# Moving two small table loads of a rotary-embedding kernel to ScalarE's DMA queue, each in three parts

## The chip, the cores and the metric

The kernel runs on one core of a Trainium2 chip. The metric is the device time of one execution in microseconds (us), as the median of several runs. The span in a profile is some 2 us shorter than that time (160.8 against 162.55 us in the profiled run of the kernel before).

## The reference, cut to what matters

```python
x = x.reshape(batch, seq, num_heads, head_dim)       # 16, 512, 16, 64; float32
x1, x2 = x[..., :32], x[..., 32:]
rotated = concatenate([x1 * cos - x2 * sin, x1 * sin + x2 * cos], axis=-1)
```

x and the result have 33.55 MB each; cos and sin have 512 x 32 values, 64 KB each. The arithmetic is small beside the 67 MB that go in and out.

## The kernel before

x is cut into 8 tiles of 128 partitions x 8,192 values (4 MB). A tile is loaded, rotated in place and stored, and SyncE (SP) issues every load and store on its own queue. Five tile buffers are used in turn. The start, where the change lies:

```python
FIRST = (3, 8)                       # tile 0 is loaded in two parts: 3 and 5 row blocks
...
load(0, 0, FIRST[0])                 # SP: x tile 0, part 1: 12,288 bytes a partition
sin_sb = bp.tile(...)[:64, :256]
cos_sb = bp.tile(...)[:64, :256]
nc.sync.dma_start(out=sin_sb, in_=sin_v)   # 64 rows of 1,024 bytes
nc.sync.dma_start(out=cos_sb, in_=cos_v)
for lo, hi in zip(FIRST, FIRST[1:]):
    load(0, lo, hi)                  # x tile 0, part 2: 20,480 bytes a partition
for t in range(1, BUFS):
    load(t)                          # x tiles 1 to 4: 32,768 bytes a partition
...
# both batches of a tile use the same 64 table rows: PE copies them to 128 partitions
nc.tensor.matmul(out=sin_t, lhsT=spread, rhs=sin_sb, ...)
nc.tensor.matmul(out=cos_t, lhsT=spread, rhs=cos_sb, ...)
nc.vector.tensor_scalar_mul(out=sns[:, :, 0, :], in0=sin_k, scalar1=-1.0)
nc.vector.tensor_copy(out=sns[:, :, 1, :], in_=sin_k)
... # then all of VectorE's and POOL's work on x, which needs both tables
```

The x products with cos and most sums are VectorE's (DVE in the profile), 7 of 8 products with sin are POOL's, and PE with ScalarE (ACT) does a quarter of the sums.

Of the kernel before, what the change touches and what calls it, by code (L numbers as in the profile page):

```python
# [27 lines left out]
def kernel(  # L28
# [13 lines left out]
    nc = tc.nc  # L42
# [12 lines left out]
    cos_v = cos.rearrange("(p k) j -> p (k j)", k=KK)  # L55
    sin_v = sin.rearrange("(p k) j -> p (k j)", k=KK)
# [22 lines left out]
    load(0, 0, FIRST[0])  # L79
    sin_sb = bp.tile([P, dim], FP32, name="b")[:PB, : KK * half]  # L80
    cos_sb = bp.tile([P, dim], FP32, name="b")[:PB, : KK * half]
    nc.sync.dma_start(out=sin_sb, in_=sin_v)
    nc.sync.dma_start(out=cos_sb, in_=cos_v)
    for lo, hi in zip(FIRST, FIRST[1:]):
        load(0, lo, hi)
    for t in range(1, BUFS):
# [27 lines left out]
    def cos_b(k, n):  # L114
        c = cos_t[:, k * half : (k + 1) * half]
        return bass.AP(tensor=c.tensor, offset=c.offset, ap=[c.ap[0], [0, n], [1, half]])
# [17 lines left out]
    def pairs(r):  # L134
        return r.rearrange("p (a j) -> p a j", j=half)
# [21 lines left out]
    for t in range(NT):  # L157
        xt = tiles[t]
        for k in range(KK):
# [6 lines left out]
            if k in PE_ROWS[t % 2]:  # L166
                parts = []
                for c in range(0, dim, BANK):
# [3 lines left out]
                        out=pairs(ps), in0=pairs(rc), in1=cos_b(k, BANK // half), op=ALU.mult  # L172
# [51 lines left out]
```

## Time and profile before

| | before |
|---|---|
| median time | 162.58 us (162.51 to 162.78, 5 runs beside the changed kernel) |
| first and last movement of data (packet records) | 1.74 and 159.37 us after the span's start |
| sin, cos landed | 7.6 and 8.0 us |
| first VectorE product on x | 10.90 us |
| last store issued | 152.1 us |

Two bounds have nearly the same height. The DMA engines always have data to move, and VectorE works without a stop from 10.90 us to its end at 152.07 us. The lines are in the prediction below. Throughout, "packet records" are the trace's list of single DMA transfers: one entry for each contiguous row (1,024, 12,288, 20,480 bytes and so on) and one of 4 bytes for each completion signal of a DMA engine. The records don't name the DMA engine; where medians over the 16 engines are given, packets of one size were taken sixteen at a time in order of start.

The times of packet records in the prediction and in the expectations were counted from a point 0.24 us before the start that the timeline uses: 1.98, 6.33 and 159.6 us there are 1.74, 6.10 and 159.4 us on the timeline's clock. Outside those texts this document gives all packet times on the timeline's clock.

### The profile page before, as it was taken

The numbers are of one execution on the slowest core, as the hardware profiler recorded it, in microseconds if no ns is written. First come the engines' busy times: TensorE is split into PE (matmuls) and PEld (weight loads), VectorE is DVE, ScalarE is ACT, GpSimd is POOL, SyncE is SP. The second block draws the span as 40 slices with busy tenths as digits, with TensorE's granted clock in tenths as the row PEclk, the third lists the DMA queues.
The fourth block names the chain that finished last, engine by engine and source line by source line (L and its number), as shares of the span: only waits on it lengthen the run. The fifth ranks groups of instructions, "written<-read, shape, count | busy, mean of one in ns | idle before, by whom it ended". The sixth has DMA issues, their size and how long they took to land. (4 is left out here: it accounts for less than half of the span.)

```text
span 160.8 us, 524 instructions
## 1 busy us (share of the span) xinstructions
PE 62.3 (39%) x71; PEld 20.0 (12%) x71; DVE 141.4 (88%) x142; ACT 20.0 (12%) x33; POOL 130.3 (81%) x62
## 2 busy tenths in 40 slices
PE   3045380546217260708035440918053721735000
PEld 0022020202011110202020200211020201111000
DVE  1059999999999999999999999999999999999800
ACT  0110220021102020111102020112002110202000
POOL 1039999999999999999999899999999799950000
PEclk9999958576956755595555555555955585587655
DMA  5999999999999999999999999999999999999994
GB/s 186 395 423 463 408 481 416 391 497 416 391 489 416 402 416 481 408 391 505 399 399 481 424 399 475 424 408 432 465 399 432 465 408 432 457 416 408 428 428 179
DMA packets 2754, 67.26 MB, mean 418 GB/s; under 512 B 320, under 2 KB 448, under 8 KB 448
## 3 DMA queue, kind: packets, MB, share of 16 engines
q1 hardware_dynamic: 2752, 67.24, 97.9%
q14 instruction: 2, 0.02, 0.0%
HBM read 33.69 MB, written 33.55 MB: 418 GB/s over the span
## 5 line engine op out<-in xcount | busy, mean ns | idle before, releaser
L165 POOL TENSOR_TENSOR b<-xt,sns 128x1024 f32<-128x1024 f32 x56 | 129.6, 2358 | 11.8 <-DVE sns L108 9.4
L183 DVE TENSOR_TENSOR pd<-xt,tab 128x1024 f32<-128x1024 f32 x48 | 58.1, 1225 | 0.8
L145 DVE TENSOR_TENSOR xt<-pd,b 128x1024 f32<-128x1024 f32 x48 | 58.4, 1218 | 0.0
L178 PE MATMUL ps<-xt,ident 128*128 128x512 f32 x32 | 29.5, 1077 | 48.6 <-issue 38.1
L178 PE MATMUL ps<-b,ident 128*128 128x512 f32 x32 | 29.4, 1073 | 29.8 <-DVE ps L171 27.1
L179 ACT COPY xt<-ps 128x512 f32<-128x512 f32 x32 | 18.7, 585 | 120.3 <-PE ps L178 120.3
L171 DVE TENSOR_TENSOR ps<-xt,tab 128x512 f32<-128x512 f32 x32 | 20.6, 688 | 0.0
L178 PEld LDWEIGHTS ps<-xt,ident 128*128 128x128 f32 x32 | 9.4, 324 | 68.2 <-issue 63.6
L178 PEld LDWEIGHTS ps<-b,ident 128*128 128x128 f32 x32 | 9.2, 316 | 49.7 <-issue 25.6
L176 DVE TENSOR_TENSOR xt<-xt,tab 128x1024 f32<-128x1024 f32 x8 | 9.8, 1221 | 0.4
L107 DVE TENSOR_SCALAR sns<-tab 128x256 f32<-128x256 f32 x1 | 0.4, 424 | 8.2 <-PE tab L105 8.2
L104 PE MATMUL tab<-b,spread 64*128 64x256 f32 x2 | 1.2, 696 | 5.1 <-DMA b<-in_sin_dram 5.1
L179 ACT ACT_TABLE_LOAD x1 | 1.3, 1283 | 7.3 <-DMA xt<-in_x_dram 7.3
L95 PE MATMUL ps<-zero 128*128 128x512 bf16 x3 | 1.5, 626 | 1.2 <-DVE zero L92 1.2
L104 PEld LDWEIGHTS tab<-b,spread 64*128 64x128 f32 x2 | 0.5, 307 | 6.0 <-issue 6.0
L105 PE MATMUL tab<-b,spread 64*128 64x256 f32 x2 | 1.1, 631 | 0.0
L92 DVE MEMSET zero<- 128x256 uint32 x1 | 0.3, 272 | 0.9 <-PEq L205 0.9
L105 PEld LDWEIGHTS tab<-b,spread 64*128 64x128 f32 x2 | 0.7, 333 | 0.2
L103 DVE COPY spread<-ident 64x64 f32<-64x64 f32 x2 | 0.3, 184 | 0.2 <-POOL ident masks.py:199 0.2
L95 PEld LDWEIGHTS <-zero 128*128 128x128 bf16 x3 | 0.3, 124 | 1.5 <-DVE zero L92 1.2
masks.py:197 POOL MEMSET ident<- 128x128 f32 x1 | 0.2, 205 | 0.3 <-POOLq L205 0.3
L108 DVE COPY sns<-tab 128x256 f32<-128x256 f32 x1 | 0.4, 414 | 0.0
(6 smaller groups left out, 0.9 us busy)
## 6 DMA issues: line engine op xcount, KB each, us to landing
xt<-in_x_dram SPq DMA_DIRECT2D x7, 4096.0 KB, 29.1
out_dram<-xt SPq DMA_DIRECT2D x7, 4096.0 KB, 23.6
out_dram<-xt SPq DMA_DIRECT2D x2, 2048.0 KB, 8.1
xt<-in_x_dram SPq DMA_DIRECT2D x1, 2560.0 KB, 11.5
xt<-in_x_dram SPq DMA_DIRECT2D x1, 1536.0 KB, 6.5
b<-in_sin_dram SPq DMA_DIRECT2D x1, 64.0 KB, 6.5
b<-in_cos_dram SPq DMA_DIRECT2D x1, 64.0 KB, 6.3
```

Of the source, the lines that this page charges most:

```text
L95: nc.tensor.matmul(out=ps, lhsT=zero[:, :P], rhs=zero, start=True, stop=True)
L104: nc.tensor.matmul(out=sin_t, lhsT=spread, rhs=sin_sb, start=True, stop=True)
L105: nc.tensor.matmul(out=cos_t, lhsT=spread, rhs=cos_sb, start=True, stop=True)
L107: nc.vector.tensor_scalar_mul(out=sns[:, :, 0, :], in0=sin_k, scalar1=-1.0)
L108: nc.vector.tensor_copy(out=sns[:, :, 1, :], in_=sin_k)
L145: nc.vector.tensor_tensor(out=r, in0=ps, in1=b, op=ALU.add)
L165: nc.gpsimd.tensor_tensor(out=halves(b), in0=swapped(r, nh), in1=over_heads(sk), op=ALU.mult)
L171: nc.vector.tensor_tensor(out=pairs(ps), in0=pairs(rc), in1=cos_b(k, BANK // half), op=ALU.mult)
L176: nc.vector.tensor_tensor(out=halves(r), in0=halves(r), in1=swapped_signed(k), op=ALU.mult)
L178: nc.tensor.matmul(out=ps, lhsT=ident, rhs=rhs, start=False, stop=True, skip_group_check=True)
L179: nc.scalar.copy(out=rc, in_=ps)
L183: nc.vector.tensor_tensor(out=pairs(ps), in0=pairs(r), in1=cos_b(k, 2 * nh), op=ALU.mult)
```

## The change

The intent is to take the tables out of SP's queue, behind whose first x part they wait, and to let the idle ScalarE issue them on its own queue in parallel. Each table is cut into parts of 32, 16 and 16 rows. The program then has 24 transfers, up from 20.

```diff
-    nc.sync.dma_start(out=sin_sb, in_=sin_v)
-    nc.sync.dma_start(out=cos_sb, in_=cos_v)
+    for sb, v in ((sin_sb, sin_v), (cos_sb, cos_v)):
+        for lo, hi in ((0, 32), (32, 48), (48, 64)):
+            nc.scalar.dma_start(out=sb[lo:hi, :], in_=v[lo:hi, :])
```

## The prediction

> **What bounds the kernel now.** I read the page's shares of the span first, then the DMA queue, then the start and the end of the timeline, because a change to two small loads at the start can only matter if the start decides when the end comes.
>
> ```profile
> PE 62.3 (39%) x71; PEld 20.0 (12%) x71; DVE 141.4 (88%) x142; ACT 20.0 (12%) x33; POOL 130.3 (81%) x62
> DMA  5999999999999999999999999999999999999994
> q1 hardware_dynamic: 2752, 67.24, 97.9%
> HBM read 33.69 MB, written 33.55 MB: 418 GB/s over the span
> ```
>
> The sixteen DMA engines hold work in every slice: 67.24 MB have to move, and the first packet of the trace's packet records starts at 1.98 us, the last ends at 159.6 us, with no hole between. That is 67.24 MB / 157.6 us = 427 GB/s. DMA is a floor, and no change of issuing engine lowers the bytes. But VectorE (DVE) is a second bound of nearly the same height, as the timeline of the start and of the end shows:
>
> ```profile
> 0.73 0.38 SPq L73 DMA_DIRECT2D xt<-in_x_dram  x1
> 1.17 0.52 SPq L82 DMA_DIRECT2D b<-in_sin_dram  x1
> 1.74 0.58 SPq L83 DMA_DIRECT2D b<-in_cos_dram  x1
> 2.36 2.61 SPq L73 DMA_DIRECT2D xt<-in_x_dram  x5
> ...
> 7.77 1.19 PE L104 MATMUL tab<-b,spread 64*128 64x256 f32 x2 [5.12 <-DMA b<-in_sin_dram]
> 8.76 1.06 PE L105 MATMUL tab<-b,spread 64*128 64x256 f32 x2
> 9.85 0.42 DVE L107 TENSOR_SCALAR sns<-tab 128x256 f32<-128x256 f32 x1 [8.22 <-PE tab L105]
> 10.69 13.90 POOL L165 TENSOR_TENSOR b<-xt,sns 128x1024 f32<-128x1024 f32 x6 [9.39 <-DVE sns L108]
> 10.90 1.29 DVE L171 TENSOR_TENSOR ps<-xt,tab 128x512 f32<-128x512 f32 x2
> ```
>
> The reader is to see a chain: sin and cos land (7.7 and 8.0 us), PE spreads them over 128 partitions, VectorE makes the signed sin table, and only then can VectorE and POOL touch x. VectorE waits 8.22 us for it. From 10.90 us on it never stops:
>
> ```profile
> 149.72 2.35 DVE L145 TENSOR_TENSOR xt<-pd,b 128x1024 f32<-128x1024 f32 x2
> ...
> L77 SPq DMA_DIRECT2D out_dram<-xt x9: 332/333/348, 31.1 to 152.1; - x9
> ```
>
> The waits of the VectorE groups after 10.8 us sum to 1.2 us in 141 us. It ends at 152.07 and the last store (2 MB) is issued at 152.1. In the packet records that store's first packets start at 153.74, straight behind the previous store's last. The first load took 1.98 - 0.73 = 1.25 us from issue to first packet, so this store could have started at 153.4. So the DMA backlog in front of the last store is worth only about 0.35 us more than its own latency. The two bounds are thus asymmetric: if VectorE starts earlier, the end stays, since the DMA still has all its bytes to move; if VectorE starts X later, the end moves by about X - 0.35, since VectorE has no idle time to catch up in.
>
> **What the Trainium skill says.** "DMA: Bandwidth & Descriptors", section "Issuing engines are not separate DMA queues": transfers from several issuing engines run on the same 16 DMA engines and interleave; only sequencer time is saved. So I count no bandwidth. The trace before has one queue (q1) for all data and can't confirm it. The same page, "Queues, rings and completion order": each DMA engine goes round robin between the queues that have work, one packet at a time. No run shows this yet; it is the step the prediction rests on. That section calls 9 to 17 descriptors a typical packet; this case's records instead list each row as a packet (12,288, 20,480, 1,024 bytes) and each completion signal as one of 4 bytes (320 = 20 transfers x 16). I take a packet to be one row or one signal. "Perfetto Trace Analysis", "DMA Instruction — HWDGE (DVE, Sync)": the issue's own span doesn't contain the data movement. The trace agrees: 0.52 us of issue for sin, 6.5 us to landing.
>
> **The change part by part.**
> *Issue.* Removed: two issues from SP (0.52 + 0.58 us). Added: six on ScalarE, which before did nothing until 7.29 us. SP's starts lie 0.44 to 0.62 us apart, mean 0.54, so ScalarE's run from about 0.75 to 0.75 + 5 x 0.54 = 3.45 us, and the last reaches the DMA engines about 1.25 us later, at 4.7. No engine is busy then: no cost.
> *Bytes.* The same 128 rows of 1 KB. Four more transfers are 64 more 4-byte packets of 0.009 us, or 0.04 us for each engine.
> *Completion counters.* The built programs use eight in turn. With 24 transfers the load of tile 1 reuses that of the first sin part, tile 2's that of the first x part, tiles 3 and 4 those of the other sin parts, so SP now waits for these landings before it issues. The x data already queued keeps the DMA busy to about 12.9 us, so these waits are hidden if sin lands by about 11. Later reuses fall on transfers long landed, or on the same store whose buffer is awaited anyhow.
> *Position.* Before, the table rows stood behind the first x part in the one queue: they ran in one burst, from 6.33 to 7.26 us. Now each engine alternates. It has 2 + 1 + 1 rows and 3 signals for sin, the same for cos: 14 turns, each behind one x packet. Those took about 1.0 us (the first), 0.467 us (12,288 bytes), 0.766 us (20,480 bytes); a table row 0.046.
> Sin: seven x packets, 1.98 + 1.0 + 6 x 0.467 + 4 x 0.046 = 6.0 us; landing 0.5 to 0.8 us later as before (last cos signal 7.25, landed 8.04): about 6.7.
> Cos: its first turn follows the eighth x packet (6.5), its second the x part's signal, the other five follow 20,480-byte packets: 6.55 + 5 x 0.766 + 3 x 0.046 = 10.5, landed about 11.3 us, against 8.0 before.
> *Sum.* The sin product is then already done; the cos product takes 1.06 us and ends at 12.4 against 9.82. X = 2.6 us, POOL and VectorE begin at about 13.3 and 13.5. End: 2.6 - 0.35 = 2.25 us later, 162.77 + 2.25 = 165.0 us.
>
> **The rivals.**
> *1. Tables early or unmoved, hidden by the DMA floor* (25%). If a signal takes no turn of its own, cos needs 8 turns, its rows end at about 6.5 us and it lands at about 7.3. VectorE then starts 1 us earlier, and nothing comes of it: 162.7 us. For it: the table rows are tiny and their queue is its own. Against it: signals are separate packets in the records.
> *2. The turns above* (50%): 165.0, from 164 to 166.2 as the turns fall.
> *3. Tables later than that* (25%): the engine takes several x rows for one turn, or x rows already read ahead stand before each turn. One extra 0.77 us row adds 0.8 us of delay; two x rows a turn over the last turns add some 4. That gives 166 to 169. The extreme, a packet being a whole transfer's share of an engine, would put the cos parts behind whole 4 MB tiles (9.7 us each) and cost tens of microseconds; I give it 4% within this.
> *Faster by over 2%* needs 3.3 us out of a DMA stream that has no hole; only its 2 us at either end are free of data, and the change touches neither. 2%.
>
> **Range and chances.** Weighting 162.7, 165.0 and about 167 to 168 by 25, 50 and 25% gives about 165; I say 164.9. The range 162.4 to 167.5 runs from rival 1 with noise to the middle of rival 3. Slower by over 2% starts at 166.03: about 15% of rival 2 and most of rival 3, together 0.29. Within 2%: 0.69. Faster: 0.02.
>
> **What would show it.** The landing of cos in the DMA issues: about 11.3 us after the start here, about 7.3 under rival 1, 12 and up under rival 3. The start of the first VectorE product of tile 0: 13.5 against 10.90; its last sum at 152.07 + 2.6 = 154.7, the last store's issue right behind. The DMA row should show a thinner slice near the end, and the DMA share of the span fall to about 96.5%. The 1,024-byte packets should be strewn between x packets from 2 to 10.5 us rather than stand in one burst. The prediction is wrong if cos lands before 9 us (then no loss), if VectorE proves able to catch up a late start, or if SP's counter waits leave the DMA empty near 13 us.

## The result, and the profile after

The changed kernel takes 166.41 us (166.33 to 166.66, 5 runs) against 162.58 us. The ratio is 1.0232, with a 95% interval of 1.0218 to 1.0246. A ratio is the mean time of one kernel's fast runs over the mean of the other's of the same rounds, so it is not quite the ratio of the medians. Executions over 1.5% slower than the fastest of the same kernel are left out of the means. The change costs 3.83 us.

The page of the changed kernel, in the lines that answer to those of before:

```profile
PE 62.7 (38%) x71; PEld 19.9 (12%) x71; DVE 141.4 (86%) x142; ACT 20.0 (12%) x33; POOL 130.3 (79%) x62
DMA  5999999989999899998999999899999999799896
q1 hardware_dynamic: 2592, 67.11, 96.7%
q10 hardware_dynamic: 224, 0.13, 0.3%
HBM read 33.69 MB, written 33.55 MB: 409 GB/s over the span
```

VectorE's busy time is unchanged at 141.4 us, so no operation became slower. There is a second queue, q10, with 224 packets: 128 rows and 96 signals. The DMA row is no longer full, and shows its thinnest slice (7) near the end. The timeline of the start:

```profile
0.73 1.35 ACTq L84 DMA_DIRECT2D b<-in_sin_dram  x3
...
2.11 1.54 ACTq L84 DMA_DIRECT2D b<-in_cos_dram  x3
...
7.95 1.19 PE L105 MATMUL tab<-b,spread 64*128 64x256 f32 x2 [5.31 <-DMA b<-in_sin_dram]
...
13.77 1.19 PE L106 MATMUL tab<-b,spread 64*128 64x256 f32 x2 [4.62 <-DMA b<-in_cos_dram]
14.99 0.42 DVE L108 TENSOR_SCALAR sns<-tab 128x256 f32<-128x256 f32 x1 [13.37 <-PE tab L106]
...
15.83 11.59 POOL L166 TENSOR_TENSOR b<-xt,sns 128x1024 f32<-128x1024 f32 x5 [14.53 <-DVE sns L109]
16.04 1.29 DVE L172 TENSOR_TENSOR ps<-xt,tab 128x512 f32<-128x512 f32 x2
```

ScalarE issues all six parts within the first 3.65 us, yet PE waits for cos until 13.77 us, where it did the same product at 8.76 us before. Sin came at about the same time as before (7.95 against 7.77 us). The first product on x starts at 16.04 us instead of 10.90, that is 5.14 us late. The view of the cos table gives its way from issue to landing, in us (least, median, most of the three parts):

```profile
L84 ACTq DMA_DIRECT2D b<-in_cos_dram x3: 477/477/525, 2.1 to 3.2; - x3
...
DMA to landing us min/median/max: 8.2/9.3/10.5
```

The last part was issued at 3.2 us and took 10.5 us. At the end of the program, the view of the stores and the two-microsecond stretches around the issue of the last one (columns after the stretch: its length, busy time and instruction count of PE, PE weight load, VectorE, ScalarE and POOL, PE clock, DMA share, GB/s). First the kernel before, then the changed one:

```profile
152.00:154.00 2.00, 0.00 (x0) 0.00 (x0) 0.07 (x1) 0.00 (x0) 0.00 (x0) 0.50 1.00 426
154.00:156.00 2.00, 0.00 (x0) 0.00 (x0) 0.00 (x0) 0.00 (x0) 0.00 (x0) 0.50 0.99 426
```

```profile
L77 SPq DMA_DIRECT2D out_dram<-xt x9: 332/333/347, 36.3 to 157.2; - x9
...
156.00:158.00 2.00, 0.00 (x0) 0.00 (x0) 1.17 (x2) 0.00 (x0) 0.00 (x0) 0.50 0.62 262
158.00:160.00 2.00, 0.00 (x0) 0.00 (x0) 0.00 (x0) 0.00 (x0) 0.00 (x0) 0.50 1.07 451
```

VectorE ends 5.1 us later than before, and the last store is issued at 157.2 instead of 152.1 us. Now the DMA engines are out of work before that store reaches them: the packet records show the previous store's signals end at 157.75 us and the last store start at 158.08 us, with nothing between. (The DMA share of a stretch counts a packet whole where it starts and is rough; the gap in the records is the evidence.) From the first product to the last store's issue it is 157.2 - 16.04 = 141.2 us, and it was 152.1 - 10.90 = 141.2 us before. The loss comes from the start, and the slack from the end: from its issue to its last packet the last store takes 7.23 us in the kernel before, behind other work on the DMA engines, and 5.91 us in the changed kernel, where they are free. The difference of 1.32 us is what a late store could absorb.

Where the table rows stood in the packet records (medians over the 16 DMA engines, us on the timeline's clock):

| turn | sin rows | sin signals | cos rows | cos signals |
|---|---|---|---|---|
| before, one queue | all rows and signals of both tables in one burst, 6.10 to 7.02 | | | |
| after, part 1 | 3.05, 3.55 | 4.05 | 7.33, 8.21 | 9.09 |
| after, part 2 | 5.49 | 5.98 | 9.86 | 10.73 |
| after, part 3 | 6.41 | 6.50 | 11.58 | 12.46 (slowest engine 13.06) |

### The profile page after: what moved, and what is told of

It reads as the page before. It is cut to its first block, busy times and chain, and to the rows that moved or that the text cites. A ratio compares the mean times of both kernels' runs of the same rounds, so it can differ in the third digit from the quotient of the medians.

```text
span 164.3 us, 532 instructions
## 1 busy us (share of the span) xinstructions
PE 62.7 (38%) x71; PEld 19.9 (12%) x71; DVE 141.4 (86%) x142; ACT 20.0 (12%) x33; POOL 130.3 (79%) x62
```

## The experiments

**The theory.** While x packets stand in SP's queue, each table row and each signal in ScalarE's queue waits for about one x packet; cos lands late; VectorE starts late and can't catch up; the end moves by the delay less a fixed slack of about 1.3 us. That slack is 5.14 - 3.83 of the result itself. **Rivals:** the number of transfers, with the reuse of completion counters that comes with it; something fixed about ScalarE's queue; a DMA that is slower later on.

### Same parts, one queue

```diff
-            nc.scalar.dma_start(out=sb[lo:hi, :], in_=v[lo:hi, :])
+            nc.sync.dma_start(out=sb[lo:hi, :], in_=v[lo:hi, :])
```

> The same six table parts and 24 transfers, but issued by SyncE in its own queue, at the place where the two table loads stood before. Theory (turns between two queues make cos late): no second queue, so the table rows run in one burst behind the first x part, cos lands at about 8.2 us after the span's start, the first product of tile 0 starts at about 11 us, and the time is that of before, 162.4 to 162.9 us. Rival (the number of transfers, the reuse of completion counters or the three parts cost the time): about 166.4 us as in the changed kernel.

Measured: 163.12 us (162.89 to 163.35) against 162.55 us, ratio 1.0036 (1.0021 to 1.0051).

```profile
8.76 1.06 PE L106 MATMUL tab<-b,spread 64*128 64x256 f32 x2
...
10.90 1.29 DVE L172 TENSOR_TENSOR ps<-xt,tab 128x512 f32<-128x512 f32 x2
```

Both lines have the very times of the kernel before. The 24 transfers, their parts and the counters are not the cause of the late tables; the second queue is. The time is 0.57 us longer than before all the same, a little above what I expected. The packet records show where but not why: the last signals of the 16 DMA engines are spread from 158.45 to 160.35 us, where before they lay between 158.36 and 159.36. Some engines finished later with the same bytes of data.

### Fewer turns: one transfer for each table on ScalarE's queue

Against the kernel before:

```diff
-    nc.sync.dma_start(out=sin_sb, in_=sin_v)
-    nc.sync.dma_start(out=cos_sb, in_=cos_v)
+    nc.scalar.dma_start(out=sin_sb, in_=sin_v)
+    nc.scalar.dma_start(out=cos_sb, in_=cos_v)
```

> ScalarE's queue, but one transfer for each table: 4 rows and 1 signal on each DMA engine for each table, 10 turns instead of 14. Theory: cos lands four turns of some 0.85 us sooner than in the changed kernel (13.7 us), at 9.3 to 10.9, the first product starts 2.3 us later (11.6 to 13.2 against 10.90 before), 0.7 to 2.3 us late, of which 1.3 us are slack: 162.6 to 163.7 us. If it is the second queue as such, whatever the turns: about 166.4 us. If only the parts matter: 162.6 us with cos at about 8.

Measured: 164.95 us (164.62 to 165.35), ratio 1.0142 (1.0124 to 1.0160).

```profile
12.34 1.22 PE L105 MATMUL tab<-b,spread 64*128 64x256 f32 x2 [3.04 <-DMA b<-in_cos_dram]
...
14.65 1.29 DVE L171 TENSOR_TENSOR ps<-xt,tab 128x512 f32<-128x512 f32 x2
```

The direction was right and the size wrong: cos landed 1.4 us sooner than with three parts, not 2.8 to 4.4. The packet records show why. The turns of cos are as expected (rows at 8.05, 8.91, 9.78 and 10.67, signal at 11.58, steps of 0.88 us), but the first table row of all came only at 4.99 us, where in the changed kernel it came at 2.50 us. So there is a second term besides the turns: a lag before a transfer's first row gets its first turn. Given the product's start, 3.75 us late, the time fits: 164.95 - 162.55 = 2.40, and 3.75 - 2.40 = 1.35 us of slack.

### A late VectorE start without touching any load

One, then four extra VectorE operations of 128x1024 were put ahead of the signed sin table in the kernel before. The results stay correct.

```diff
+    scratch = fixed.tile([P, dim], FP32)
+    nc.vector.memset(scratch, 0.0)
+    for i in range(1):        # 4 in the second run
+        nc.vector.tensor_tensor(
+            out=pairs(scratch), in0=cos_b(0, 2 * nh), in1=pairs(scratch), op=ALU.mult)
     nc.vector.tensor_scalar_mul(out=sns[:, :, 0, :], in0=sin_k, scalar1=-1.0)
```

> The kernel before with one more VectorE operation of 128x1024 (some 1.2 us) ahead of the signed sin table; tables and queues as before. Theory (VectorE has no idle time to catch up in, and the store backlog at the end gives 1.3 us of slack): first product 1.2 us late, all of it absorbed, 162.5 to 162.9 us. My slack of the prediction (0.35 us) would give 163.4 us.

Measured: 162.49 us (162.37 to 162.56), ratio 0.9997 (0.9982 to 1.0011).

```profile
11.84 1.30 DVE L177 TENSOR_TENSOR ps<-xt,tab 128x512 f32<-128x512 f32 x2
```

The first product started at 11.84 us, 0.94 us late (the tables happened to land 0.2 us sooner), and nothing of it reached the end. A slack of 0.35 us would have cost 0.6 us.

> The kernel before with four more VectorE operations of 128x1024 (some 4.8 us together) ahead of the signed sin table. Theory (a late start of VectorE alone makes the loss of the changed kernel): first product 4.7 to 4.9 us late, less 1.3 us of slack: 165.9 to 166.3 us. Rival (the second queue slows the DMA itself later on): the delay is caught up or costs clearly less than in the changed kernel, under 165 us.

Measured: 165.96 us (165.66 to 166.21), ratio 1.0210 (1.0195 to 1.0225).

```profile
9.39 5.00 DVE L117 TENSOR_TENSOR scratch<-tab,scratch 128x1024 f32<-128x1024 f32 x4 [6.69 <-PE tab L105]
...
15.35 1.29 DVE L177 TENSOR_TENSOR ps<-xt,tab 128x512 f32<-128x512 f32 x2
```

The product is 15.35 - 10.90 = 4.45 us late and the time 3.41 us longer: a slack of 1.04 us. (The profiled execution was the fastest of the four, 165.66 us, so this slack comes out small.) With one queue and the old loads, a late VectorE alone makes a loss like that of the change. A DMA slowed later on is not needed to explain it.

### Larger x packets beside the six parts

```diff
-FIRST = (3, 8)
+FIRST = (8,)
```

> The changed kernel, with tile 0 loaded in one transfer, so that every x packet is 32,768 bytes (1.21 us) instead of 12,288 and 20,480. Theory (each table row and each signal waits for one x packet): 14 turns and some two lost ones of 1.26 us each, cos lands at 22 to 24 us, the first product starts at 24 to 26.5 us, and the time is 162.6 + 13 to 15.6 - 1.3, that is 174 to 177 us. Rival (ScalarE's queue adds a fixed delay of some 10 us, whatever the x packets): cos lands at about 14 us as in the changed kernel, about 167 us.

Measured: 172.68 us (172.48 to 173.01), ratio 1.0621 (1.0603 to 1.0640).

```profile
20.11 1.19 PE L106 MATMUL tab<-b,spread 64*128 64x256 f32 x2 [6.58 <-DMA b<-in_cos_dram]
...
22.38 1.29 DVE L172 TENSOR_TENSOR ps<-xt,tab 128x512 f32<-128x512 f32 x2
```

The tables, their queue and their issue are those of the changed kernel; only the rows of x beside them are longer. PE has cos at 20.1 instead of 13.8 us. The signals of the six parts stand at 6.33, 8.93, 11.52, 14.17, 16.73 and 19.28 us: steps of 2.6 us are two turns of 1.3 us, just over the 1.21 us of one 32,768-byte packet. The first cos part has two rows and yet fits in such a step, because its rows (12.61 and 12.85 us) have only the 4-byte signal of x tile 0 between them (12.78 us), which also counts as a turn. A fixed delay of ScalarE's queue falls with this. I expected some two lost turns more and got none, so the landing came 2 us below my range. The product is 11.48 us late, the time 10.08 us longer: 1.40 us of slack.

### Smaller x packets beside ScalarE's queue

Against the kernel before (the table issues also stand behind tile 0's loads in the program now, but they are on another engine):

```diff
-FIRST = (3, 8)
+FIRST = (1, 2, 3, 4, 5, 8)      # 4,096-byte packets first
...
-    nc.sync.dma_start(out=sin_sb, in_=sin_v)
-    nc.sync.dma_start(out=cos_sb, in_=cos_v)
+    nc.scalar.dma_start(out=sin_sb, in_=sin_v)
+    nc.scalar.dma_start(out=cos_sb, in_=cos_v)
```

> ScalarE's queue with one transfer for each table, and x tile 0 loaded as five transfers of one row block (4,096-byte packets, some 0.16 us) and one of the rest. Theory: ten turns of 0.2 us, cos lands at 4.5 to 6 us, sooner than before the change (8.0), the first product starts at 7 to 8.5 us, and as the DMA is then the only bound, nothing is gained: 162.3 to 163.0 us. Rival (ScalarE's queue is slow as such): cos after 9 us. Rival (a sooner start of VectorE is worth time): 160.5 us or less.

Measured: 162.64 us (162.59 to 162.77), ratio 1.0003 (0.9988 to 1.0018).

```profile
6.88 1.22 PE L105 MATMUL tab<-b,spread 64*128 64x256 f32 x2 [0.49 <-DMA b<-in_cos_dram]
...
9.19 1.29 DVE L171 TENSOR_TENSOR ps<-xt,tab 128x512 f32<-128x512 f32 x2
```

With the same queue the tables now land sooner than in the kernel before: cos is there at 6.88 us, and all rows of a table follow one another within some 0.5 us (sin 3.70 to 4.15). ScalarE's queue is not slow as such. The first product comes 1.71 us sooner than before, a little later than I expected, and the time doesn't change. That is the other half of the argument: an earlier VectorE gains nothing. Cos came 0.9 us later than the range expected, so the turns alone don't tell when a table lands; the lag before its first row is again in it (first row at 3.70 us, issue at 0.73).

### Tables first in SP's queue

```diff
-    load(0, 0, FIRST[0])
     sin_sb = ...; cos_sb = ...
     nc.sync.dma_start(out=sin_sb, in_=sin_v)
     nc.sync.dma_start(out=cos_sb, in_=cos_v)
+    load(0, 0, FIRST[0])
```

> The kernel before, with sin and cos issued by SyncE ahead of the first x part. Theory: tables land at about 3.5 us, x part one at about 8, the first product starts at about 8 us, near 3 us sooner than before; the x stream starts up to 0.6 us later behind the two small transfers. DMA is the only bound then: 162.4 to 163.3 us. Rival (VectorE's start sets the end, with no DMA floor): 159.9 us.

Measured: 163.86 us (163.79 to 164.07), ratio 1.0081 (1.0064 to 1.0098).

```profile
4.01 1.06 PE L105 MATMUL tab<-b,spread 64*128 64x256 f32 x2
...
8.45 1.29 DVE L171 TENSOR_TENSOR ps<-xt,tab 128x512 f32<-128x512 f32 x2 [2.32 <-DMA xt<-in_x_dram]
```

VectorE starts 2.45 us sooner, and the program ends 1.26 us later, 0.6 us beyond my range. In the packet records the data starts at 2.06 instead of 1.74 us, and after that the engines stand idle for 0.89 us of the first 5 us, against 0.18 before. Together that is 1.03 us of work not done early, of the 1.23 us by which the last packet ends later: a DMA that has no free time passes such a loss on. The remaining 0.2 us is open. The expectation had counted the later start ("up to 0.6 us") but not the idle engines behind two small transfers.

### Is the lag before a part made by SP's second load?

In the changed kernel the second sin part's row came 5.49 - 4.05 = 1.44 us after the first part's signals, where a turn took 0.50 us (the expectation says 0.46, the time of the x packet alone). One candidate was SP's second x load, issued at about the same time as that part. It was held back by a dependency:

```diff
+    c = FIRST[0] * dim
+    nc.vector.tensor_copy(out=tiles[0][:32, c : c + 1], in_=sin_sb[:32, :1])
     for lo, hi in zip(FIRST, FIRST[1:]):
         load(0, lo, hi)
```

> The changed kernel, with SyncE's second x load held back until the first sin part has landed (a one-column VectorE copy into the tile makes it wait), so that for the first 5 us only one x load stands beside the six table parts. In the changed kernel the row of the second sin part came 1.4 us after the signals of the first, where one turn is 0.46 us. If the second part's descriptors are made behind those of SyncE's second x load (one generator for both), its rows now follow within one turn, at about 4.3 to 4.9 us instead of 5.7. If the lag comes from something else (x rows already read ahead, or a slow start of each part under load), they stay at 5.3 to 6.0. No claim is made on the time; the DMA may run dry for about 1 us.

Measured in a single look (state unknown): the second part's row stays at 5.46 us (5.70 in the expectation's count), so SP's second load doesn't make the lag. The time, of which nothing was claimed, was 164.71 us against 162.77. The run shows something more useful: the first x load is over at about 6.5 us, and all the remaining table rows and signals then ran in a burst, from 6.3 to 6.9 us. (The time is longer because of something else than VectorE's start; the x stream has gaps near 7 us here, and the rest was not looked into.)

```profile
8.60 1.06 PE L108 MATMUL tab<-b,spread 64*128 64x256 f32 x2
...
10.75 1.29 DVE L174 TENSOR_TENSOR ps<-xt,tab 128x512 f32<-128x512 f32 x2
```

With the six parts on ScalarE's queue, but no x packets beside their second half, the product starts as early as in the kernel before (10.75 against 10.90 us).

### Are the places of the rows the same from run to run?

> The changed kernel once more, to see whether the places of the table rows are the same from run to run: medians for the 16 engines of 3.3, 3.8, 5.7, 6.6, 7.6, 8.4, 10.1 and 11.8 us for the eight rows if they are set by the program, others by 0.5 us and more if the two queues race at the start. Time 166.0 to 166.8 us.

Measured: rows at 3.05, 3.62, 5.52, 6.49, 7.38, 8.27, 9.90 and 11.54 us (0.24 us more in the expectation's count), all within 0.1 us of the first time; 166.38 us.

> The run with one transfer for each table on ScalarE's queue once more: its first table row came only after seven x packets (5.2 us), where the changed kernel's first part came after one or two (2.7 us). If that is a property of the larger transfer: again near 5.2 us and cos landed near 12.3 us. If the two queues race at the start: the first row at about 2.7 to 3.3 us, and cos landed at about 10 us. Time 164.6 to 165.3 or, in the second case, 162.6 to 163.3 us.

Measured: first row at 5.12 us (5.36 in the expectation's count), PE's cos product at 12.15 us; 164.83 us. Both repeats agree with the first. The lag belongs to the program and is not a race that falls differently each time. What makes it, I did not find.

### All runs on one scale

| run | first product | late by X | time against before | X less that |
|---|---|---|---|---|
| tables first | 8.45 | -2.45 | +1.26 | |
| small x packets | 9.19 | -1.71 | +0.04 | |
| same parts, one queue | 10.90 | 0 | +0.57 | |
| one extra operation | 11.84 | 0.94 | -0.06 | absorbed |
| whole tables, two queues | 14.65 | 3.75 | +2.40 | 1.35 |
| four extra operations | 15.35 | 4.45 | +3.41 | 1.04 |
| the change | 16.04 | 5.14 | +3.83 | 1.31 |
| large x packets | 22.38 | 11.48 | +10.08 | 1.40 |

Times are medians less the median of the kernel before of the same rounds. X comes from one profiled execution and the time from all of them, so the last column is good to some tenths. At X = 0.94 us and below the DMA set the end; from 3.75 us up VectorE's start did, and between the two nothing was measured. From 5.14 to 11.48 us the time grew by 6.25 us for 6.34 us of delay. The traces confirm the slack of about 1.3 us: in the profiled runs of the change, of four extra operations and of the large x packets, the last store took 5.91, 5.91 and 5.92 us from issue to its last packet, against 7.23 us in the kernel before. No run is faster than the kernel before by more than the noise.

## Why the prediction was right or wrong, point by point

- **Two bounds, of which only a later VectorE costs time: right.** Late starts made without any second queue were absorbed (0.94 us) or passed on less the slack (4.45 us), and earlier starts gained nothing.
- **Turns between two queues: right as a mechanism.** Rows of 1,024 bytes and signals of 4 bytes both take turns with x packets, and the turn follows the x packet's size: 0.50, 0.86 and 1.3 us beside 12,288, 20,480 and 32,768 bytes.
- **The landing of cos: mis-sized.** The step "10.5, landed about 11.3 us" measured 13.77 us at PE. Three terms of it were off. The first cos row came at 7.33 us instead of 6.26 (6.5 in the prediction's count), since two turns were lost ahead of the second sin part; sin, due at 6.7, landed at 7.8 us. The cos turns then fell beside six 20,480-byte packets, 0.86 us a turn and 5.13 us in all, instead of five of 0.766 and some small rows, 3.97 us. And the slowest of the 16 DMA engines ran 0.6 us behind the median, and PE started on cos 1.31 us after the median's last signal, instead of 1.04 (0.8 in the prediction's count). The differences are 1.07 + 1.16 + 0.27 = 2.5 us. My rival 3 named late turns with the wrong picture for the first term (several x rows in every turn); they were lost at one place.
- **X: 2.6 us predicted, 5.14 us measured,** and the excess is that of cos: PE's cos product and what follows it took 2.3 us to the first product, where the prediction implied 2.2.
- **The slack of 0.35 us: wrong, it is about 1.3 us.** I took the first load's time from issue to first packet (1.00 us; 1.25 in the prediction's count) and the start of the last store on the first DMA engine that came free. When the engines are free that store needs 158.08 - 157.25 = 0.83 us, but what counts at the end is the slowest engine. From issue to the last packet of all the store took 7.23 us before and 5.91 us in the changed kernel, and the difference, 1.32 us, is the slack.
- **The sum** was therefore 2.25 us where 3.83 us came; the two errors partly cancelled. That is luck: with the true slack and my X, I would have said 162.6 + 2.6 - 1.3 = 163.9 us. The range held 166.41 us, but the result is past the 2% line, to which I gave 0.29. The range and the chance of "slower" rested on rival 3, and it was there that the result fell (cos at 12 us and up).
- **The packet clock: misread by 0.24 us.** Issue and packet times were set beside each other with packets 0.24 us too late. In the slack and in the landing of cos the slip entered twice with opposite signs, so no predicted time changes.
- **SP's counter waits hidden: right.** The engines show no idle time near 13 us, and the same parts on one queue kept VectorE's start.

## What to carry to other kernels

In this kernel a small load on a second queue didn't run ahead of a large one: it took turns with it, one row or one signal for each row of the large load, so count its rows and signals on one DMA engine and multiply by the time of the neighbour's row. In the change and with whole tables that count came out too low: a lag before a transfer's first row came on top (0.9 us before the second sin part, more with whole tables), which the runs don't explain. In one queue, a small load behind a short large one may land sooner, because nothing stands between its rows. And before one moves a start, one should ask both ways what it is worth: here an earlier start was worth nothing, and a later one cost its whole length beyond about 1.3 us.

## What the Trainium skill lacked or had wrong

- "DMA: Bandwidth & Descriptors", "Queues, rings and completion order": it says that an engine goes round robin by packet, which these runs bear out, and gives 9 to 17 descriptors as a typical packet. Here the turn was a single row or a single 4-byte signal (the records don't show into how many descriptors a row is cut): 14 turns for a table pair in six parts, with a step of 2.6 us for each pair of turns beside 32,768-byte packets.
- Same page, "Issuing engines are not separate DMA queues": it says that issuing from several engines only saves issue time. It lacks that the interleaving can cost time: a small transfer moved to the second queue landed 5 us later (13.77 against 8.76 us at PE) and took the kernel from 162.58 to 166.41 us.
- Same page, "Latency and other measured facts": it gives some 600 ns to the first byte of a transfer issued by SP or ScalarE, without saying from where it counts. On the idle queue here the first packet came 1.00 us after the issue began and 0.62 us after it ended (issue 0.73 to 1.11, first packet at 1.74), so the figure fits the second count. It lacks what a busy neighbour does: beside a running x load the first row of the sin table came 2.3 us after the issue began (first of three parts: 0.73, then 3.05) and 4.6 us (whole table: 0.73, then 5.30), medians over the engines. The runs leave open what this depends on.
- No page gives the size of this: with DMA as the bound, the 16 engines don't end together. Their last signals lay 1.0 us apart in the kernel before and 1.9 us with six parts in the same queue. Where VectorE was the bound they lay 0.15 us apart in the changed kernel, but 0.6 us in the profiled run with whole tables, and the slowest sets the end.
